# Chunked delta rule: preparing the next head block by block, in the order in which the last head's scan frees its tiles

## The chip, the cores and the metric

One of the eight cores of a Trainium2 chip runs the whole program in one launch. The metric is the device time of one execution in microseconds. TensorE (PE in the profile) multiplies matrices into the eight banks of PSUM; VectorE (DVE), ScalarE (ACT) and GpSimdE (POOL) do elementwise work; SyncE (SP) issues the DMAs.

## What is computed

The reference is a backbone of two layers over 256 context tokens and 1024 latent tokens, model width 1024, all in float32. Each layer has a mixer (one input projection, three groups of heads, one output projection) and a squared-ReLU MLP of width 4096. The three groups are a gated delta rule (GDN, four heads of 128, both directions), an RG-LRU (a linear recurrence, both directions) and latent attention (four heads). The change is in the GDN, which the reference computes like this for each head and direction:

```
G = jnp.cumsum(g, axis=-1)
decay = jnp.exp(jnp.where(incl, G[..., :, None] - G[..., None, :], -jnp.inf))
low = jnp.where(strict, jnp.einsum('nbhid,nbhjd->nbhij', kb, k) * decay, 0.0)
amat = low + jnp.eye(GDN_CHUNK, dtype=low.dtype)
sol = lax.linalg.triangular_solve(amat, rhs, left_side=True, lower=True, unit_diagonal=True)
attn = jnp.einsum('nbhid,nbhjd->nbhij', q, k) * decay
qg = q * jnp.exp(G)[..., None]

def step(S, inp):
    u_i, w_i, a_i, qg_i, kg_i, gl_i = inp
    v_new = u_i - jnp.einsum('bhcd,bhde->bhce', w_i, S)
    o_i = jnp.einsum('bhcd,bhde->bhce', qg_i, S) + jnp.einsum('bhij,bhje->bhie', a_i, v_new)
    S = S * gl_i[..., None, None] + jnp.einsum('bhcd,bhce->bhde', kg_i, v_new)
    return S, o_i
```

## The kernel before

The kernel cuts the 1280 tokens into three blocks: `c` (256 context tokens), 0 and 1 (512 each). For the GDN it uses chunks of 128 tokens, ten of them: 0 and 1 are block `c`, 2 to 5 block 0, 6 to 9 block 1. It is written as straight Python that traces every instruction; a scheduler then puts each engine's instructions into one fixed queue, roughly by their place in the program and by when it expects their inputs to be ready. On the chip each engine works through its queue in order and waits on semaphores. So the order of work is settled before the run, and an instruction that waits holds back what is queued behind it on its engine.

In the mixer (`mixer`), `tiles(h)` projects k, q, v and the gate z of GDN head h: each projected tile is 24 TensorE matmuls of up to 512 columns for each block (`mm3`, L230), a convolution on VectorE, and transpositions into the bank `st` (L443, L462). k, q and v go to memory. `head(h)` then runs the head. The program order is tiles(0), head(0), tiles(1), head(1), tiles(2), head(2), the two RG-LRU projections, tiles(3), head(3), and last the projections of the latent attention (`kvq`). Then come `mla_open` and `mla_prep` (attention's keys, queries and maxima: L950, L958, L984, in banks `st` and `b`), the RG-LRU (`lru`, 20 segments, L847 in bank `lr`), `mla_attend` (L1014 to L1029) and the output projection.

A head has four stages:

- preparation (`gdn_head`, before `gdn_invert`): for each block the decays of both directions (transpositions L624 into banks `a` and `b`, a masked addition on VectorE, exponentials on ScalarE), k·k (L636) into bank `c`, scaled into the triangles `N`, k·q (L646) into bank `c` again, multiplied into the chunk attention `at`, and q scaled by its decay (`Qg`, on GpSimdE);
- inversion (`gdn_invert`): the triangles of all chunks and both directions together. L676 and copies collect 32x32 diagonal blocks in `C`; L681 transposes `C` into `X` on VectorE; 30 pairs of small VectorE instructions follow, then L690 and the small products of L696;
- scan (`gdn_scan`): ten steps in which both directions advance by a chunk. The forward direction takes chunks 0 to 9, the backward one 1, 0, 9, 8, ..., 2. Each step has five products (L766 to L790, banks `a`, `b` and `c`). The output is summed in `o`, which lies in the buffer of `X`; k in token order lies in that of `C`, the states in that of `X2`;
- output (`gdn_y`): squares, a reciprocal root, scaling, transpositions (L821, banks `a`, `b`, `c`), the product with the gate, a store.

Every large tile of a head (`kT`, `qT`, `vt`, `N0`, `N1`, `at0`, `at1`, `Qg1`, `C`, `X`, `X2`) is taken anew for each head from a single buffer (`g5`, `bufs=1`), so that a head's tile takes the place of the last head's. The tiles `L` of the RG-LRU have 14 buffers; a segment takes five.

Of the kernel before, what the change touches and what calls it, by code (L numbers as in the profile page):

```python
# [7 lines left out]
F32 = mybir.dt.float32  # L8
F32R = mybir.dt.float32r
I32 = mybir.dt.int32  # L10
AF = mybir.ActivationFunctionType
ALU = mybir.AluOpType
# [4 lines left out]
P = 128  # L17
# [3 lines left out]
CTX = 256  # L21
TOK = CTX + SEQ
NCH = TOK // P
# [8 lines left out]
BL = ["c", 0, 1]  # L32
# [11 lines left out]
class Trunk:  # L44
# [540 lines left out]
        self.gv8 = ("G", "nG", "neG", "eGl")  # L585
        self.gv = dict(beta=beta, nbeta=nbeta, G=G, nG=nG, neG=neG, eGl=eGl, bk=bk)

    def g5(self, tag):
        return self.gp.tile([P, TOK], F32, tag=tag, bufs=1, name=self.nm(tag))

    def gdn_head(self, L, h, kss, qss, vd, last):

        nc = self.nc
        (kd, ssk, ktd), (qd, _, _) = kss, qss
        y, t, hv, rt, r2 = [self.small([P, NCH], "hk", 6) for _ in range(5)]
        self.rsqrt(y, ssk, t, hv)
        self.tt(rt, ssk, y, ALU.mult)
        self.tt(r2, y, y, ALU.mult)  # L600
        gv = dict(self.gv)
        hc8 = self.small([P, 3, NCH, 2], "hc8", 2)
        for i, k in enumerate(("nbeta", "beta", "bk")):
            gv[k] = hc8[:, i]
            self.tt(hc8[:, i], self.gv[k][:, :, h:8:4], r2.rearrange("p (c o) -> p c o", o=1).to_broadcast([P, NCH, 2]), ALU.mult)
        qbl = [0, 1] if last else BL
        kT, qT, vt = self.g5("kT"), self.g5("qT"), self.g5("vt").rearrange("p (c d) -> p c d", d=P)
        q0 = CTX if last else 0
        nc.sync.dma_start(kT, kd)
        nc.sync.dma_start(qT[:, q0:], qd[:, q0:])  # L610
        nc.sync.dma_start(vt, vd.rearrange("p (c d) -> p c d", d=P))
        self.tt(vt, vt, rt.rearrange("p (c o) -> p c o", o=1).to_broadcast([P, NCH, P]), ALU.mult, nc.gpsimd)
        N = [self.g5(f"N{d}").rearrange("p (c i) -> p c i", i=P) for d in range(2)]
        at = [self.g5(f"at{d}").rearrange("p (c i) -> p c i", i=P) for d in range(2)]
        Qg = [qT, self.g5("Qg1")]
        for b in BL:
            c0, w = GRP[b]
            qs = slice(c0 * P, (c0 + w) * P)
            x = None
            for d in range(2):  # L620
                hc = 4 * d + h
                bc = self.PT("ab"[d]).rearrange("p (c i) -> p c i", i=P)
                for i in range(w):
                    nc.tensor.transpose(bc[:, i, :], gv["G"][:, c0 + i, hc:hc + 1].to_broadcast([P, P]), self.ident)  # L624
                E = at[d][:, c0:c0 + w, :]
                self.tt(E, bc[:, 0:w, :], self.mask[d].rearrange("p (o i) -> p o i", o=1).to_broadcast([P, w, P]), ALU.add)
                for i in range(w):
                    self.act(E[:, i, :], E[:, i, :], AF.Exp, bias=gv["nG"][:, c0 + i, hc:hc + 1])
                if b in qbl:
                    if d == 0:  # L630
                        x = self.T()[:, :w * P]
                    self.act(Qg[1][:, qs] if d else x, bc[:, 0:w, :].rearrange("p c i -> p (c i)"), AF.Exp)
            pk = self.PT("c").rearrange("p (c i) -> p c i", i=P)
            for i in range(w):
                cs = slice((c0 + i) * P, (c0 + i + 1) * P)
                nc.tensor.matmul(pk[:, i, :], kT[:, cs], kT[:, cs], start=True, stop=True)  # L636
            for i in range(w):
                for d in range(2):
                    hc = 4 * d + h
                    c = c0 + i  # L640
                    self.stt(N[d][:, c, :], pk[:, i, :], gv["nbeta"][:, c, d:d + 1], at[d][:, c, :], ALU.mult, ALU.mult)
            if b in qbl:
                pq = self.PT("c").rearrange("p (c i) -> p c i", i=P)
                for i in range(w):
                    cs = slice((c0 + i) * P, (c0 + i + 1) * P)
                    nc.tensor.matmul(pq[:, i, :], kT[:, cs], qT[:, cs], start=True, stop=True)  # L646
                for d in range(2):
                    self.tt(at[d][:, c0:c0 + w, :], pq[:, 0:w, :], at[d][:, c0:c0 + w, :], ALU.mult)
                self.tt(Qg[1][:, qs], qT[:, qs], Qg[1][:, qs], ALU.mult, nc.gpsimd)
                self.tt(qT[:, qs], qT[:, qs], x, ALU.mult, nc.gpsimd)  # L650
        self.gdn_invert(N)
        return self.gdn_scan(h, gv, kT, ktd, vt, N, at, Qg, last)

# [5 lines left out]

    def gdn_invert(self, N):  # L660

# [7 lines left out]
        for a in range(4):  # L669
            q = slice(32 * a, 32 * a + 32)  # L670
            self.cp2(a, C[q, 0:NCH, :], N[0][q, :, 32 * a:32 * a + 32])
        pc = self.PT('a').rearrange("p (c i) -> p c i", i=32)
        for a in range(4):
            q = slice(32 * a, 32 * a + 32)
            for c in range(NCH):
                nc.tensor.matmul(pc[q, c, :], N[1][q, c, 32 * a:32 * a + 32], self.ident[q, 32 * a:32 * a + 32],  # L676
                                 start=True, stop=True, tile_position=(32 * a, 32 * a))
# [148 lines left out]
    def lru(self, L, xd, gd, blocks, yd):  # L826

        nc = self.nc
        gp = nc.gpsimd
        hd = [self.dram(f"lh{t}") for t in range(2)]  # L830
        W = 256
# [1 line left out]
        y0 = GRP[blocks[0]][0] * P  # L833

        def R():
            return self.mp.tile([P, W], F32, tag="L", bufs=14, name=self.nm("lr"))
        prev = {}

        def segment(d, t, b):
            i = 2 * d + t  # L840
            ini = prev.get((d, t), 0.0)
            cs = slice(b * W, (b + 1) * W)
            u = R()
            nc.sync.dma_start(u, xd[t][:, cs])
            ps = self.PT("lr").rearrange("p (g n) -> p g n", g=2)
            for g in range(2):
                nc.tensor.matmul(ps[:, g, :], self.lw[:, d, g, t, :], u, start=True, stop=True)  # L847
            r, wh, y, q = R(), R(), R(), R()

            self.act(r, ps[:, 0, :], AF.Exp, bias=L.col("lba", i))  # L850
# [184 lines left out]
    def mixer(self, L, hs, obl):  # L1035

        nc = self.nc
        l, last = L.l, L.l == DEPTH - 1
        pk = {}
# [4 lines left out]
        d = pk["krba"] = self.dram("krba")  # L1044
# [21 lines left out]
        gp = self.gp = self.pool("gp", other)  # L1066
        self.XAT = gp.tile([P, NCH, 64], F32, name=self.nm("XAT"))
        nc.gpsimd.memset(self.XAT, 0.0)
        kd, xg = [], []

        def tiles(h):
# [362 lines left out]
```

## Time and profile before

| what | us |
|---|---|
| median of three runs | 3839.47 |
| fastest and slowest of them | 3834.44, 3847.36 |
| the profiled execution, its own time | 3835.08 |
| its span, first to last instruction | 3833.3 |
| TensorE busy (91% of the span) | 3505.4 |
| VectorE busy (55%) | 2106.1 |
| ScalarE busy (43%) | 1648.3 |
| GpSimdE busy (34%) | 1314.7 |

The profile is of one execution. A line of its timeline gives the start in us from the span's start, the duration, the engine, the line of the program, the operation, the tiles (written, then read), the shapes, a count of merged instructions and, in brackets, the idle time before it and what ended it. A line of its groups gives a count, the busy time, the mean duration in ns, and the idle time ahead of the group with its causes. PSUM banks appear as `pa`, `pb`, `pc`, `pd`, `pst`, `plr` and `mm`. A float32 product of 128x128 by 128x128 shows as two records. The ends of matmuls are modelled, so that a busy TensorE may in part be a waiting one.

### The profile page before, as it was taken

What the parts mean: (1) busy time and instruction counts of PE and PEld (TensorE: products, weight loads), DVE (VectorE), ACT (ScalarE), POOL (GpSimd) and SP (SyncE); (2) the same over time, 40 slices, a digit from 0 to 9 for tenths busy, and PEclk for the clock granted to TensorE, in tenths of its full rate; (3) what the DMA queues carried; (4) which work ended last, traced back from release to release, by engine and by line L of the source; (5) the groups of instructions that cost most, each with busy time, mean ns of one, the idle gap of its engine ahead of it and who ended that gap; (6) DMA issues with size and microseconds to landing.
All of it is one profiled execution on the core that took longest, in us unless ns stands there. A gap on an engine that the chain in (4) does not pass through costs nothing. (4 is left out here: it accounts for less than half of the span.)

```text
span 3833.3 us, 51463 instructions
## 1 busy us (share of the span) xinstructions
PE 3505.4 (91%) x19236; PEld 2741.0 (72%) x19236; DVE 2106.1 (55%) x4351; ACT 1648.3 (43%) x3477; POOL 1314.7 (34%) x919
## 2 busy tenths in 40 slices
PE   5999898798998999999997989996798999999998
PEld 3777687344687888888877777774455778888886
DVE  6667757666265155555266587677576371421124
ACT  3555464455454322212354455544555453222242
POOL 4211311335475211111466321113334674222253
PEclk9999999898999999999998999997798999999998
DMA  5221222232432222232334222212002433311143
GB/s 182 94 83 66 83 97 76 91 100 64 151 105 88 67 83 94 88 94 89 128 109 138 99 81 82 77 65 87 31 24 74 153 107 94 96 47 46 52 139 99
DMA packets 164922, 347.13 MB, mean 91 GB/s; under 512 B 15552, under 2 KB 74304, under 8 KB 164672
## 3 DMA queue, kind: packets, MB, share of 16 engines
q1 hardware_dynamic: 164672, 343.85, 27.6%
q8 instruction: 151, 2.47, 0.3%
q14 instruction: 99, 0.81, 0.1%
HBM read 277.99 MB, written 65.80 MB: 90 GB/s over the span
## 5 line engine op out<-in xcount | busy, mean ns | idle before, releaser
L138 POOL TENSOR_TENSOR wl<-wr,wh 128x1024 fp32r<-128x1024 f32 x280 | 679.9, 2429 | 1664.2 <-ACT wh L135 931.0
L230 PE MATMUL mm<-A,wh 128*128 128x512 f32 (+1 forms) x3008 | 709.9, 379 | 12.3 <-DVE A L138 6.3
L135 ACT ACTIVATE wh<-wr 128x1024 fp32r<-128x1024 f32 x288 | 304.8, 1058 | 833.0 <-PE mm L230 328.1
L230 PEld LDWEIGHTS mm<-A,wh 128*128 128x128 f32 x3008 | 522.9, 194 | 108.0 <-ACT A L135 8.1
L138 DVE TENSOR_TENSOR hid<-T,hid 128x512 fp32r<-128x512 f32 (+1 forms) x160 | 173.1, 1084 | 448.4 <-ACT hid L135 448.4
L230 PE MATMUL mm<-A,wl 128*128 128x512 f32 (+1 forms) x1504 | 360.8, 373 | 1.5 <-DVE wl L138 1.4
L230 PE MATMUL mm<-hid,wh 128*128 128x512 f32 (+1 forms) x1280 | 302.9, 378 | 8.8 <-ACT T L135 6.8
L230 PEld LDWEIGHTS mm<-A,wl 128*128 128x128 f32 x1504 | 259.8, 191 | 48.0 <-DVE wl L138 1.6
L230 PEld LDWEIGHTS mm<-hid,wh 128*128 128x128 f32 x1280 | 227.8, 191 | 57.1 <-ACT T L135 7.3
L147 DVE SCALAR_TENSOR_TENSOR T<-raw,sm,T 128x512 f32<-128x512 f32 (+4 forms) x240 | 182.1, 760 | 45.4 <-ACT raw L135 24.2
L138 DVE TENSOR_TENSOR acc<-acc,mm 128x512 f32<-128x512 f32 (+1 forms) x140 | 88.5, 632 | 214.9 <-PE mm L230 214.2
L230 PE MATMUL pd<-A,wh 128*128 128x512 f32 (+1 forms) x704 | 193.9, 403 | 0.0
L230 PE MATMUL plr<-A,wh 128*128 128x512 f32 (+1 forms) x800 | 185.2, 382 | 0.0
L135 ACT ACTIVATE T<-T 128x512 f32<-128x512 f32 (+1 forms) x243 | 141.6, 583 | 95.2 <-DVE T L147 69.2
L1029 PE MATMUL pd<-Pt,V 128*128 128x512 f32 (+1 forms) x336 | 170.0, 628 | 10.6 <-ACT Pt L135 9.0
L138 POOL TENSOR_TENSOR S<-S,T 128x512 f32<-128x512 f32 (+1 forms) x126 | 163.4, 1299 | 36.7 <-ACT T L135 33.0
L230 PE MATMUL mm<-hid,wl 128*128 128x512 f32 (+1 forms) x640 | 167.2, 379 | 8.1 <-DVE wl L138 8.1
L230 PE MATMUL pb<-A,wh 128*128 128x512 f32 (+1 forms) x800 | 173.0, 367 | 1.2 <-ACT wh L135 1.2
L147 DVE SCALAR_TENSOR_TENSOR ada<-wa,sil,ada 128x256 f32<-128x256 f32 x392 | 168.4, 493 | 7.1 <-DMA wa<-in_w_ada_dram 7.1
L230 PEld LDWEIGHTS plr<-A,wh 128*128 128x128 f32 x800 | 143.6, 188 | 31.2
L230 PE MATMUL plr<-hid,wh 128*128 128x512 f32 (+1 forms) x640 | 153.4, 381 | 13.0 <-DVE hid L138 9.9
L147 DVE SCALAR_TENSOR_TENSOR lr<-lr,lr 128x256 f32<-128x256 f32 x218 | 107.0, 501 | 96.7 <-POOL lr L138 87.6
(365 smaller groups left out, 6843.5 us busy)
## 6 DMA issues: line engine op xcount, KB each, us to landing
wr<-in_w_mlp_dram SPq DMA_DIRECT2D x208, 512.0 KB, 3.5
wa<-in_w_ada_dram SPq DMA_DIRECT2D x96, 512.0 KB, 3.7
wr<-in_w_in_dram SPq DMA_DIRECT2D x48, 512.0 KB, 3.6
wr<-in_w_out_dram SPq DMA_DIRECT2D x32, 512.0 KB, 3.7
A<-y SPq DMA_DIRECT2D x32, 256.0 KB, 3.2
xm<-acc SPq DMA_DIRECT2D x32, 256.0 KB, 3.5
x<-xm SPq DMA_DIRECT2D x16, 512.0 KB, 6.2
kT<-k SPq DMA_DIRECT2D x8, 640.0 KB, 4.2
```

What stands on the lines that cost most here:

```text
L135: return self.nc.scalar.activation(out, in_, f, **kw)
L138: return (eng or self.nc.vector).tensor_tensor(out, a, b, op=op)
L147: return self.nc.vector.scalar_tensor_tensor(out, a, s, b, op0=op0, op1=op1)
L230: mm = nc.tensor.matmul(ps, w[wi][:, wk, :], a[:, ai, :], start=n == 0, stop=n == last)
L1029: nc.tensor.matmul(po, V[:, c, :], p, start=ci == 0, stop=ci == len(chunks) - 1)
```

## The change

The triangles `N`, the chunk attention `at` and the scaled queries `Qg` become tiles of the whole mixer, taken once for each layer and used by all four heads. A head's preparation is cut into six units, one for each block and direction, and these are written in the order (c, forward), (c, backward), (0, forward), (1, backward), (0, backward), (1, forward). Each unit loads its own part of q into `Qg`, makes its decays in bank `lr`, its own k·k in bank `st` and its own k·q in bank `lr`; before, k·k and k·q were made once for both directions. `kT` gets two buffers, `vt` is loaded and scaled after the units, and the RG-LRU's tiles have 10 buffers in place of 14.

```diff
-    def g5(self, tag):
-        return self.gp.tile([P, TOK], F32, tag=tag, bufs=1, name=self.nm(tag))
+    def g5(self, tag, bufs=1):
+        return self.gp.tile([P, TOK], F32, tag=tag, bufs=bufs, name=self.nm(tag))
...
-        kT, qT, vt = self.g5("kT"), self.g5("qT"), self.g5("vt").rearrange("p (c d) -> p c d", d=P)
...
-        nc.sync.dma_start(kT, kd)
-        nc.sync.dma_start(qT[:, q0:], qd[:, q0:])
-        nc.sync.dma_start(vt, vd.rearrange("p (c d) -> p c d", d=P))
...
-        Qg = [qT, self.g5("Qg1")]
-        for b in BL:
...
-                bc = self.PT("ab"[d]).rearrange("p (c i) -> p c i", i=P)
...
-            pk = self.PT("c").rearrange("p (c i) -> p c i", i=P)
...
-                pq = self.PT("c").rearrange("p (c i) -> p c i", i=P)
...
+        kT, vt = self.g5("kT", 2), self.g5("vt").rearrange("p (c d) -> p c d", d=P)
+        N, at, Qg = self.gNAQ
+
+        def unit(b, d):
+
             c0, w = GRP[b]
             qs = slice(c0 * P, (c0 + w) * P)
+            hc = 4 * d + h
+            if b in qbl:
+                nc.sync.dma_start(Qg[d][:, qs], qd[:, qs])
+            bc = self.PT("lr").rearrange("p (c i) -> p c i", i=P)
+            for i in range(w):
+                nc.tensor.transpose(bc[:, i, :], gv["G"][:, c0 + i, hc:hc + 1].to_broadcast([P, P]), self.ident)
+            E = at[d][:, c0:c0 + w, :]
+            self.tt(E, bc[:, 0:w, :], self.mask[d].rearrange("p (o i) -> p o i", o=1).to_broadcast([P, w, P]), ALU.add)
+            for i in range(w):
+                self.act(E[:, i, :], E[:, i, :], AF.Exp, bias=gv["nG"][:, c0 + i, hc:hc + 1])
+            if b in qbl:
+                x = self.T()[:, :w * P]
+                self.act(x, bc[:, 0:w, :].rearrange("p c i -> p (c i)"), AF.Exp)
+            pk = self.PT("st").rearrange("p (c i) -> p c i", i=P)
             for i in range(w):
                 cs = slice((c0 + i) * P, (c0 + i + 1) * P)
                 nc.tensor.matmul(pk[:, i, :], kT[:, cs], kT[:, cs], start=True, stop=True)
             for i in range(w):
+                c = c0 + i
+                self.stt(N[d][:, c, :], pk[:, i, :], gv["nbeta"][:, c, d:d + 1], at[d][:, c, :], ALU.mult, ALU.mult)
             if b in qbl:
+                pq = self.PT("lr").rearrange("p (c i) -> p c i", i=P)
                 for i in range(w):
                     cs = slice((c0 + i) * P, (c0 + i + 1) * P)
+                    nc.tensor.matmul(pq[:, i, :], kT[:, cs], Qg[d][:, cs], start=True, stop=True)
+                self.tt(E, pq[:, 0:w, :], E, ALU.mult)
+                self.tt(Qg[d][:, qs], Qg[d][:, qs], x, ALU.mult, nc.gpsimd)
+        nc.sync.dma_start(kT, kd)
+
+        for b, d in (("c", 0), ("c", 1), (0, 0), (1, 1), (0, 1), (1, 0)):
+            unit(b, d)
+        nc.sync.dma_start(vt, vd.rearrange("p (c d) -> p c d", d=P))
+        self.tt(vt, vt, rt.rearrange("p (c o) -> p c o", o=1).to_broadcast([P, NCH, P]), ALU.mult, nc.gpsimd)
         self.gdn_invert(N)
...
-            return self.mp.tile([P, W], F32, tag="L", bufs=14, name=self.nm("lr"))
+            return self.mp.tile([P, W], F32, tag="L", bufs=10, name=self.nm("lr"))
...
+        self.gNAQ = [[self.g5(f"{k}{d}") for d in range(2)] for k in ("N", "at", "Qg")]
+        self.gNAQ[:2] = [[t.rearrange("p (c i) -> p c i", i=P) for t in ts] for ts in self.gNAQ[:2]]
```

More of the change, by code (lines that the diff above doesn't have):

```diff
@@ L606, in gdn_head @@
         qbl = [0, 1] if last else BL
-        kT, qT, vt = self.g5("kT"), self.g5("qT"), self.g5("vt").rearrange("p (c d) -> p c d", d=P)
-        q0 = CTX if last else 0
-        nc.sync.dma_start(kT, kd)
-        nc.sync.dma_start(qT[:, q0:], qd[:, q0:])
-        nc.sync.dma_start(vt, vd.rearrange("p (c d) -> p c d", d=P))
-        self.tt(vt, vt, rt.rearrange("p (c o) -> p c o", o=1).to_broadcast([P, NCH, P]), ALU.mult, nc.gpsimd)
-        N = [self.g5(f"N{d}").rearrange("p (c i) -> p c i", i=P) for d in range(2)]
@@ L614, in gdn_head @@
-        at = [self.g5(f"at{d}").rearrange("p (c i) -> p c i", i=P) for d in range(2)]
-        Qg = [qT, self.g5("Qg1")]
-        for b in BL:
+        kT, vt = self.g5("kT", 2), self.g5("vt").rearrange("p (c d) -> p c d", d=P)
+        N, at, Qg = self.gNAQ
+        def unit(b, d):
             c0, w = GRP[b]
             qs = slice(c0 * P, (c0 + w) * P)
-            x = None
-            for d in range(2):
-                hc = 4 * d + h
-                bc = self.PT("ab"[d]).rearrange("p (c i) -> p c i", i=P)
[L623 to L632, printed above, removed]
-            pk = self.PT("c").rearrange("p (c i) -> p c i", i=P)
@@ L637, in gdn_head @@
             for i in range(w):
[L638 to L641, printed above, removed]
+                c = c0 + i
+                self.stt(N[d][:, c, :], pk[:, i, :], gv["nbeta"][:, c, d:d + 1], at[d][:, c, :], ALU.mult, ALU.mult)
             if b in qbl:
-                pq = self.PT("c").rearrange("p (c i) -> p c i", i=P)
+                pq = self.PT("lr").rearrange("p (c i) -> p c i", i=P)
                 for i in range(w):
                     cs = slice((c0 + i) * P, (c0 + i + 1) * P)
[L646 to L650, printed above, removed]
+                    nc.tensor.matmul(pq[:, i, :], kT[:, cs], Qg[d][:, cs], start=True, stop=True)
[6 more added lines that the diff above has]
+        self.tt(vt, vt, rt.rearrange("p (c o) -> p c o", o=1).to_broadcast([P, NCH, P]), ALU.mult, nc.gpsimd)
         self.gdn_invert(N)
```

## The prediction

> **What bounds the kernel now.** I read the page first: the engines' shares, then the forty slices.
>
> ```profile
> span 3833.3 us, 51463 instructions
> PE 3505.4 (91%) x19236; PEld 2741.0 (72%) x19236; DVE 2106.1 (55%) x4351; ACT 1648.3 (43%) x3477; POOL 1314.7 (34%) x919
> ...
> PE   5999898798998999999997989996798999999998
> ```
>
> TensorE (PE) is busy 91% of the span, and, counting slices of 95.8 us from 0, its dips lie in 4 to 12 and 21 to 30, the deepest in 27 and 28: the mixers of layer 0 and layer 1, where the four GDN heads run one after another. The rest is projection matmuls back to back, which the change doesn't touch. So I read the mixers stage by stage, in the timeline, for where the scan of one head ends (the last sum into `o`, DVE L138 `X<-X,pc`) and where the inversion of the next begins (the DVE transposition L681).
>
> ```profile
> 2321.81 0.29 DVE L138 TENSOR_TENSOR X<-X,pc 128x128 f32<-128x128 f32 x1 [1.17 <-PE pc L790]
> 2337.38 0.41 PE L821 MATMUL pb<-cst,X 128*128 128x128 f32 x1
> 2337.58 0.64 PE L624 MATMUL pa<-cst,gv 128*128 128x128 f32 x2
> 2357.75 2.09 DVE L681 STREAM_TRANSPOSE X<-C 128x1024 f32<-128x1024 f32 x1 [1.05 <-POOL qT L138]
> ...
> 2450.77 0.29 DVE L138 TENSOR_TENSOR X<-X,pc 128x128 f32<-128x128 f32 x1 [0.85 <-PE pc L790]
> 2489.70 2.09 DVE L681 STREAM_TRANSPOSE X<-C 128x1024 f32<-128x1024 f32 x1 [1.06 <-POOL qT L138]
> ...
> 2585.76 0.29 DVE L138 TENSOR_TENSOR X<-X,pc 128x128 f32<-128x128 f32 x1 [0.15 <-PE pc L790]
> 2613.89 2.10 DVE L681 STREAM_TRANSPOSE X<-C 128x1024 f32<-128x1024 f32 x1 [1.06 <-POOL qT L138]
> ```
>
> In layer 1 the gaps from scan to inversion are 36, 39 and 28 us. In the first, the last transposition of `gdn_y` (L821) starts at 2337.38, and the decays of the next head (L624, into bank `a`) only after it: the next head's preparation stands wholly in the gap. What this costs at the end shows in the table of stretches (after the length: busy time of PE, PE's weight loads, DVE, ACT and POOL with the number of instructions, then the granted clock and the DMA share):
>
> ```profile
> 2620.00:2760.00 140.00, 77.64 (x554) 53.94 (x553) 98.35 (x239) 68.64 (x184) 53.05 (x68) 0.70 0.17 55
> 2760.00:2980.00 220.00, 201.33 (x682) 119.94 (x681) 144.76 (x246) 117.05 (x238) 88.43 (x104) 0.93 0.15 46
> ```
>
> While head 3 of layer 1 inverts and scans (2620 to 2760), PE has 77.6 us of work in 140: the projection tiles have run out, and attention waits for the head.
>
> ```profile
> PE pa L821 <- ACT X L135: 12.0, 1, 12.0
> ...
> 2737.61 0.63 PE L950 MATMUL pb<-kvn,wk 128*64 128x256 f32 x1
> ```
>
> Its keys (L950) need bank `b`, which the scan and `gdn_y` of head 3 hold, and resume at 2737.61, behind a transposition of `gdn_y` (L821) that waited 12.0 us for ScalarE at the head of TensorE's queue. There a shorter chain of heads is worth time. In layer 0 it is not so:
>
> ```profile
> 267.49 0.29 DVE L138 TENSOR_TENSOR X<-X,pc 128x128 f32<-128x128 f32 x1 [1.39 <-PE pc L790]
> 304.33 2.09 DVE L681 STREAM_TRANSPOSE X<-C 128x1024 f32<-128x1024 f32 x1 [1.05 <-POOL qT L138]
> ...
> 521.78 0.29 DVE L138 TENSOR_TENSOR X<-X,pc 128x128 f32<-128x128 f32 x1 [0.22 <-PE pc L790]
> 562.15 0.38 PE L624 MATMUL pa<-cst,gv 128*128 128x128 f32 x2
> ```
>
> Head 2 ends at 522 and head 3 begins at 562: for 40 us no head runs, since its projections (`tiles(3)`) aren't there.
>
> **The change, part by part.**
>
> *The gap.* Four of six units (block and direction) can run while the last scan still works on the others, if a tile's parts are freed one by one. For reading this is so already:
>
> ```profile
> 291.06 0.43 PE L676 MATMUL pa<-cst,N 32*32 32x32 f32 x8
> 296.95 2.16 DVE L147 SCALAR_TENSOR_TENSOR N<-pc,hc,at 128x128 f32<-128x128 f32 x8
> ```
>
> L676 reads the first chunks of `N` 6 us before its last ones are written. What stays in the gap is the longer of two things: the units of the last blocks, and the release of `X` (the scan's `o`) by `gdn_y`, 2337.8 − 2321.8 = 16.0 us. I take 18 us for a gap. Gained in layer 1: 18 + 21 + 10 = 49 us. Bounds: 0 if nothing starts early; 103 − 3 × 9 = 76 if `gdn_y` shrinks to half as well.
>
> *The scan.* The moved units lengthen it. Groups of instructions (count, busy us, mean ns), and the stretch of one scan:
>
> ```profile
> L147 DVE SCALAR_TENSOR_TENSOR N<-pc,hc,at 128x128 f32<-128x128 f32 x160 | 44.0, 343 | 10.9 <-PE pc L636 8.6 <-ACT at L135 1.1 <-ACT Qg L135 0.9
> L135 ACT ACTIVATE at<-at,gv 128x128 f32<-128x128 f32 x160 | 51.7, 391 | 11.4 <-DVE at L138 11.3
> L138 DVE TENSOR_TENSOR at<-pc,at 128x512 f32<-128x512 f32 (+1 forms) x40 | 23.6, 631 | 14.3 <-PE pc L646 14.2
> L138 DVE TENSOR_TENSOR at<-pa,cst 128x512 f32<-128x512 f32 (+1 forms) x24 | 14.3, 594 | 10.9 <-PE pa L624 10.9
> L135 ACT ACTIVATE T<-pa 128x512 f32<-128x512 f32 (+1 forms) x20 | 10.7, 537 | 0.0
> ...
> 2288.60:2321.80 33.20, 33.20 (x230) 29.57 (x231) 16.38 (x47) 16.60 (x51) 2.79 (x2) 1.00 0.14 35
> ```
>
> Four units are 12 chunks: on DVE 12 × 0.343 + 4 × (0.631 + 0.594) = 9.0 us, on ACT 12 × 0.391 + 4 × 0.537 = 6.8 us. Each engine is busy half of the scan (16.4 and 16.6 of 33.2), so most of the 15.8 us falls into idle time; I take 5 us a scan, 15 for three, between 0 and 47.
>
> *Doubled products.* k·k and k·q are made once for each direction: 160 + 144 PE records more.
>
> ```profile
> 295.87 1.05 PE L636 MATMUL pc<-kT 128*128 128x128 f32 x8
> ...
> L636 PE MATMUL pc<-kT 128*128 128x128 f32 x160 | 22.8, 281 | 1.2 <-DVE at L138 1.0
> L646 PE MATMUL pc<-qT,kT 128*128 128x128 f32 x144 | 19.3, 275 | 0.0
> ```
>
> Eight follow each other in 1.05 us, the last lasting 0.28: 0.11 us each, 33.5 us for 304. Inside a scan they are covered: PE is busy there by the profile, but mostly with waiting, as its projection matmuls (L230) show in the stretches of that line alone:
>
> ```profile
> 2288.60:2321.80 33.20, 19.39 (x54) 9.45 (x55) 1.00 0.14 35
> 2321.80:2357.80 36.00, 23.57 (x75) 14.03 (x75) 0.91 0.30 108
> ...
> 267.80:304.30 36.50, 26.12 (x111) 17.19 (x110) 1.00 0.38 142
> 522.10:561.90 39.80, 33.95 (x161) 26.52 (x160) 1.00 0.40 136
> ```
>
> 54 in 33 us of scan against 161 in 39.8 us alone. If that cover is gone, all 33.5 us count.
>
> *One bank in place of two.* Decays and k·q now share `lr`, k·k has `st`, which the projection tiles use too. A head with no scan before it (head 0; head 3 of layer 0) makes its units one behind the other: the bank is held by the addition, the exponential and the product, 0.594 + 0.537 + 0.631 = 1.8 us by their groups above, so some 2 us more for each of the three blocks: 6 us (an estimate), between 0 and 12. In layer 1 that is +6 on the chain.
>
> The decays of before do alternate between banks `a` and `b`, and a row of L624 above writes `a`. The Trainium skill, "Perfetto Trace Analysis", Matmuls, asks for just this: independent matmul groups should rotate through different PSUM banks, so that one is emptied while the next is filled. By that rule every head's preparation would grow as head 0's does, 8 × 6 = 48 us in place of the 10 that the sum below charges, and the result would be 3823 + 38 = 3861, about where rival C ends. No run shown here has the one-bank form.
>
> *Loads.* q comes in 6 pieces (4 in layer 1) for each head in place of one, 32 issues more on SP.
>
> ```profile
> L610 SPq DMA_DIRECT2D qT<-q x8: 319/351/457, 130.2 to 2584.8; - x8
> DMA to landing us min/median/max: 3.4/5.3/6.8
> ```
>
> At 0.35 us that is 11 us of SP over eight heads. A piece waits for the scan's last read of its part, and weight loads queue behind it; since it lands within 5.3 us and k·q is wanted only by the scan, I put this at 0, at most one landing a head on PE (8 × 5.3 = 42) if PE reaches k·q first. `kT` with two buffers can load during the last scan, and `vt`, now asked for after the units, is first needed by the scan, so the whole inversion covers it: 0 for both; without that cover `vt` would cost its landing, some 5 us by the row of q, a head.
>
> *RG-LRU's buffers, 14 to 10.* A segment takes five tiles, so 10 still hold two segments, and two is what the queue of SP shows, each next load issued right behind a store of the segment two before:
>
> ```profile
> 2688.64 0.32 SPq L883 DMA_DIRECT2D lh<-lr  x1
> 2689.06 0.38 SPq L844 DMA_DIRECT2D lr<-lx  x1
> ```
>
> I take 0; at worst each of 20 segments waits for that store to land, 3.4 us by the quickest landing in the row of q: 0 to 68 us, beside attention.
>
> *To the end of layer 1.* At head 3's end the chain is 49 − 15 − 6 = 28 us earlier. But RG-LRU then loses alone-time: the tiles that ran in the gaps (75 L230 in 36 us) still have to run, so it starts some 9 us later, and attention 28 us earlier; at 15 us a segment (20 loads issued in 290.7 us) about three segments move into attention.
>
> ```profile
> L844 SPq DMA_DIRECT2D lr<-lx x20: 319/410/608, 2628.9 to 2919.6; - x20
> 2760.00:2980.00 220.00, 12.28 (x44) 7.88 (x44) 46.03 (x101) 44.72 (x100) 69.15 (x90) 0.93 0.15 46
> ```
>
> The second row counts only RG-LRU's instructions: 11 segments (44 PE records, four each) cost DVE 46.0 us, 4.2 each, and DVE is 66% busy there (144.8 of 220): 0.66 × 4.2 × 3 = 8 us. So −20 us at the end of layer 1, between −28 and 0.
>
> *Layer 0.* Heads 0 to 2 end about 23 us earlier (two gaps, 19 and 20, less two scans at 5 and 6 for head 0), but the 40 us without a head show that this waits for projections. Two gaps give up 39 us at 111 L230 in 36.5 us, 118 records, of which the longer scans and head 0's preparation take back some 32; 86 records at 161 in 39.8 us are 21 us. So `tiles(3)` comes out even, and head 3's 6 us, partly beside the last projections, leave +4, between −15 and +12.
>
> The sum: −20 + 4 = −16 us against the profiled execution's 3835.08, 3819. That execution is 4.4 below the median of 3839.47, so the median goes to 3823, 0.43% faster. About 0.3% (11.5 us) is what a measurement of this kernel can tell from no change.
>
> **The rivals.**
>
> *A: all of it arrives.* If scans don't stretch and layer 0's tiles keep pace, layer 1 gives −35 and layer 0 −10: about 3794. For it: DVE and ACT idle half of each scan. Against it: the 40 us of layer 0 without a head.
>
> *B: the gain is given back.* Head 3 ends earlier, but RG-LRU ends when it did, and the last loads for the output projection wait for it: layer 1 at −3, layer 0 at +4, about 3840, no change. For it: the 290.7 us of its loads reach to 2919.6, 60 us before attention ends at 2980. Against it: its engines are not full.
>
> *C: slower, by the parked bank.* k·k of the next unit needs only `kT`, so it can be put into `st` long before the scan frees its part of `at`, and sit there. Then the projection tiles' transpositions, which have no bank but `st`, wait, and TensorE in order behind them. Units of the third and fourth place wait for step 5 of ten, the last two for step 9: up to 25 us a scan. At 54 L230 lost per 33 us of scan and 161 regained per 39.8, 25 us cost 10 us a head, 60 for six heads; about 40 where tiles decide, against the 20 of layer 1: near 3860. It decides from about 8 us of parking a scan, where its 3 us for each of six heads eat the 16. For it: `st` is the tiles' only bank. Against it: tiles of the next head are done before its units.
>
> *D: the parts aren't freed one by one,* and nothing starts early: head 0's 6 us for eight heads less what is hidden, +25: 3865. Against it: L676 above.
>
> **How the numbers follow.** The forecast (3805 to 3828) gets 0.40, A 0.12, B 0.24, C 0.17, D 0.07. Faster: 0.52; no change: 0.24; slower: 0.24. The likeliest is the forecast, 3823. The range reaches to A and C, 3790 to 3862; the forecast's own is 3805 to 3828.
>
> **What would show it.** Right: k·k of the next head between L770s of the last scan; the gaps in layer 1 near 18 us; scans near 38; L950 resuming near 2710; head 3 of layer 0 starting where it did. Wrong: gaps as long as before (D); PE waits on the tiles' transpositions that grow in the scans (C); attention starting earlier and the output projection not (B). What would upset the sum most is the order that a new static schedule gives to in-order queues: one wait like L821's is 12 us.

## The result: 0.9% slower, and the profile after

The changed kernel takes 3876.27 us, the kernel before 3840.22 us on the same chip: ratio 1.0090, 95% interval 1.0075 to 1.0105. Forecast were 3823 us, 0.43% faster, and a range to 3862; the time lies above the range. The profiled execution of the changed kernel took 3874.43 us, with a span of 3872.7. Its page, the same rows as shown of before:

```profile
span 3872.7 us, 52200 instructions
PE 3542.8 (91%) x19540; PEld 2778.6 (72%) x19540; DVE 2103.4 (54%) x4351; ACT 1646.4 (43%) x3477; POOL 1311.4 (34%) x919
...
PE   5999989798999999999997989997698999999998
```

The second set of products is there, 304 more records on PE (19540 against 19236; two records are one product), the other engines are as they were, and the dips of the slices still lie in the two mixers. So the loss has to be found by stage. In the line numbers of the changed kernel everything behind the new `gdn_head` stands four lines higher (L681 is L677, and so on); its k·k is L630, its k·q L638, its decays L619.

*The gaps of layer 1*, from the last sum of a scan into `o` to the start of the inversion (timeline of VectorE, changed kernel):

```profile
2361.22 0.29 DVE L138 TENSOR_TENSOR X<-X,pc 128x128 f32<-128x128 f32 x1 [1.17 <-PE pc L786]
2396.55 2.03 DVE L677 STREAM_TRANSPOSE X<-C 128x1024 f32<-128x1024 f32 x1 [0.79 <-ACT C L135]
...
2492.55 0.29 DVE L138 TENSOR_TENSOR X<-X,pc 128x128 f32<-128x128 f32 x1 [1.41 <-PE pc L786]
2529.16 2.03 DVE L677 STREAM_TRANSPOSE X<-C 128x1024 f32<-128x1024 f32 x1 [0.79 <-ACT C L135]
...
2622.64 0.29 DVE L138 TENSOR_TENSOR X<-X,pc 128x128 f32<-128x128 f32 x1 [1.17 <-PE pc L786]
2656.36 1.92 DVE L677 STREAM_TRANSPOSE X<-C 128x1024 f32<-128x1024 f32 x1
```

35.3, 36.6 and 33.7 us, where 18 were forecast and 36, 39 and 28 stood before: nothing is gained. The reason shows in the first scan of layer 0, which runs to 277 us (timeline, first unit of the next head):

```profile
256.77 0.38 PE L619 MATMUL plr<-cst,gv 128*128 128x128 f32 x2
257.18 0.43 DVE L138 TENSOR_TENSOR at<-plr,cst 128x256 f32<-128x256 f32 x1 [1.15 <-PE plr L619]
260.16 0.59 DVE L147 SCALAR_TENSOR_TENSOR N<-pst,hc,at 128x128 f32<-128x128 f32 x2
261.07 0.61 PE L630 MATMUL pst<-kT 128*128 128x128 f32 x4
...
281.15 0.19 ACT L135 ACTIVATION_READ_ACCUMULATOR T<-X 128x1 f32 x1
281.36 0.32 SPq L814 DMA_DIRECT2D T<-z  x1
290.07 0.38 SPq L814 DMA_DIRECT2D T<-z  x1
293.42 0.38 ACT L135 ACTIVATE T<-plr 128x256 f32<-128x256 f32 x1
293.85 0.71 PE L638 MATMUL plr<-Qg,kT 128*128 128x128 f32 x4
...
298.31 0.64 DVE L147 SCALAR_TENSOR_TENSOR N<-pst,hc,at 128x128 f32<-128x128 f32 x2 [0.47 <-ACT at L135]
```

The unit starts in the scan as it should: decays at 256.77, mask at 257.18, `N` at 260.16, so the parts of `at` and `N` are freed one by one. Then its exponential `x` (`T<-plr`) comes 36 us later. `x` takes one of two scratch tiles of the head's actor, and `gdn_y` of the last head holds these for its squares (to 281.15) and its `z` (loads issued at 281.36 and 290.07); e1 below tests whether it is this wait. Until `x` has read it, bank `lr` is parked, and behind it all other units; the k·k of the second unit sits in bank `st` from 261.07 to 298.31, when its `N` is made. The units then follow each other in the gap.

*Layer 0* lost more. The last transposition of head 3's projection tiles (L462) and the first decays behind it, before and after, and the projection matmuls (L230) in the stretch up to there (length, busy time of PE with the count, weight loads, granted clock, DMA share):

```profile
554.19 0.65 PE L462 MATMUL pst<-cst,T 128*128 128x128 f32 x4
...
58.00:554.80 496.80, 347.88 (x1481) 246.89 (x1482) 0.96 0.24 82
```

```profile
570.26 0.66 PE L462 MATMUL pst<-cst,T 128*128 128x128 f32 x4
578.22 0.38 PE L619 MATMUL plr<-cst,gv 128*128 128x128 f32 x2
...
58.00:570.90 512.90, 343.86 (x1481) 247.76 (x1482) 0.97 0.26 84
```

In both kernels exactly 1481 projection records stand ahead of head 3, and head 3 follows the last transposition by some 7 us. The same projections take 16.1 us longer. Between them stand the products of heads 0 to 2 (groups of TensorE by form in the same stretches, before and after):

```profile
L636 PE MATMUL pc<-kT 128*128 128x128 f32 x60 | 8.5, 280 | 1.1 <-DVE at L138 1.0
L646 PE MATMUL pc<-qT,kT 128*128 128x128 f32 x60 | 8.2, 275 | 0.0
```

```profile
L630 PE MATMUL pst<-kT 128*128 128x128 f32 x120 | 17.2, 277 | 0.3 <-DVE N L147 0.3
L638 PE MATMUL plr<-Qg,kT 128*128 128x128 f32 x120 | 17.1, 282 | 1.2 <-ACT T L135 1.2
```

120 records more at the prediction's 0.11 us are 13.2 of the 16.1 us. Head 3 itself then runs into RG-LRU. RG-LRU's matmuls within its scan (the stretch runs from the scan's first product to the end of its last sum into `o`), before and after:

```profile
626.70:666.20 39.50, 2.22 (x8) 1.29 (x8) 1.00 0.37 123
```

```profile
654.20:703.50 49.30, 4.14 (x12) 2.02 (x12) 0.93 0.24 74
```

Twelve RG-LRU matmuls in place of eight, the first 19 us into the scan in place of 31, and a scan of 49.3 in place of 39.5 us. Attention of layer 0 starts at 751.7 in place of 723.2 and, of the same length, ends 28.6 us later.

### The profile page after: what moved, and what is told of

The parts are those of the page before. It is cut to its first block, busy times and chain, and to the rows that moved or that the text cites. A ratio compares the mean times of both kernels' runs of the same rounds, so it can differ in the third digit from the quotient of the medians.

```text
span 3872.7 us, 52200 instructions
## 1 busy us (share of the span) xinstructions
PE 3542.8 (91%) x19540; PEld 2778.6 (72%) x19540; DVE 2103.4 (54%) x4351; ACT 1646.4 (43%) x3477; POOL 1311.4 (34%) x919
## 3 DMA queue, kind: packets, MB, share of 16 engines
q1 hardware_dynamic: 169280, 348.57, 28.1%
## 5 line engine op out<-in xcount | busy, mean ns | idle before, releaser
L230 PE MATMUL mm<-A,wh 128*128 128x512 f32 (+1 forms) x3008 | 703.9, 376 | 15.2 <-DVE A L138 7.7
L230 PEld LDWEIGHTS mm<-A,wh 128*128 128x128 f32 x3008 | 520.6, 192 | 111.3 <-DVE A L138 9.2
L230 PE MATMUL mm<-A,wl 128*128 128x512 f32 (+1 forms) x1504 | 352.9, 372 | 1.4 <-DVE wl L138 1.4
L230 PE MATMUL mm<-hid,wh 128*128 128x512 f32 (+1 forms) x1280 | 302.2, 377 | 5.7 <-ACT T L135 4.0
L230 PEld LDWEIGHTS mm<-A,wl 128*128 128x128 f32 x1504 | 260.4, 191 | 49.6 <-DVE wl L138 1.6
L230 PEld LDWEIGHTS mm<-hid,wh 128*128 128x128 f32 x1280 | 227.9, 191 | 53.1 <-ACT T L135 4.4
L230 PE MATMUL pd<-A,wh 128*128 128x512 f32 (+1 forms) x704 | 197.4, 411 | 1.5 <-ACT T L135 1.0
L1025 PE MATMUL pd<-Pt,V 128*128 128x512 f32 (+1 forms) x336 | 166.7, 617 | 21.1 <-ACT Pt L135 13.8
L230 PE MATMUL plr<-A,wh 128*128 128x512 f32 (+1 forms) x800 | 185.3, 383 | 0.0
L230 PE MATMUL mm<-hid,wl 128*128 128x512 f32 (+1 forms) x640 | 166.9, 379 | 8.1 <-DVE wl L138 8.1
L230 PE MATMUL pb<-A,wh 128*128 128x512 f32 (+1 forms) x800 | 173.0, 367 | 1.2 <-ACT wh L135 1.2
L230 PEld LDWEIGHTS plr<-A,wh 128*128 128x128 f32 x800 | 143.6, 188 | 31.3
L230 PE MATMUL plr<-hid,wh 128*128 128x512 f32 (+1 forms) x640 | 153.2, 381 | 12.8 <-DVE hid L138 10.0
L230 PEld LDWEIGHTS pb<-A,wh 128*128 128x128 f32 x800 | 136.8, 190 | 27.5 <-ACT wh L135 1.3
```

The source lines that it names most:

```text
L230: mm = nc.tensor.matmul(ps, w[wi][:, wk, :], a[:, ai, :], start=n == 0, stop=n == last)
L1025: nc.tensor.matmul(po, V[:, c, :], p, start=ci == 0, stop=ci == len(chunks) - 1)
```

## Experiments

All times are ratios to the kernel before on the same chip, and 0.1% is 3.8 us. The stages are read from one profile each. Layer 0 is the same code in before, e9, e14 and e15, and its attention ended at 1003.4, 1003.5, 1008.6 and 1013.0 us: in layer 0 a difference under 10 us between two profiles says nothing by itself. In the table, "head 3" is the first decay of head 3 in layer 0, "end 0" the last value product of layer 0's attention, and layer 1 is counted from a mark shortly ahead of it, the last long wait in layer 0's MLP (the product `mm<-hid,wl` that starts after 8 us of idle TensorE, at 2080.9 before), to the first score of attention, and from there to the last value product.

| kernel | ratio | head 3 | end 0 | layer 1: to attention + attention = sum |
|---|---|---|---|---|
| before | 1 | 562.2 | 1003.4 | 680.3 + 219.3 = 899.6 |
| after | 1.0090 | 578.2 | 1032.0 | 689.2 + 219.6 = 908.8 |
| e1 own x | 1.0095 | 579.8 | 1033.9 | 666.2 + 240.0 = 906.2 |
| e2 doubled only | 1.0066 | 580.1 | 1029.9 | 663.2 + 239.5 = 902.7 |
| e3 buffers only | 1.0012 | 562.2 | 1005.6 | 680.0 + 220.8 = 900.8 |
| e4 own x, banks a, b, c | 1.0081 | 586.9 | 1044.2 | 654.4 + 239.9 = 894.3 |
| e5 after, single | 1.0129 | 587.1 | 1044.2 | 692.3 + 219.9 = 912.2 |
| e6 own x, single | 1.0040 | 577.7 | 1036.5 | 639.3 + 238.2 = 877.5 |
| e7 tiles(3) first | 1.0002 | 540.0 | 1017.5 | 665.1 + 229.1 = 894.2 |
| e8 e4 with tiles(3) first | 1.0054 | 528.3 | 1034.2 | 631.3 + 265.5 = 896.8 |
| e9 shared, layer 1 | 0.9970 | 561.0 | 1003.5 | 642.5 + 239.6 = 882.1 |
| e10 shared, both layers | 1.0019 | 573.4 | 1033.0 | 642.8 + 240.7 = 883.5 |
| e11 no products | 1.0037 | 571.7 | 1012.9 | 678.7 + 218.6 = 897.3 |
| e12 loads only | 1.0007 | 566.1 | 1011.9 | 679.1 + 217.9 = 897.0 |
| e13 own x, bank lr | 1.0150 | 580.7 | 1047.4 | 681.2 + 237.6 = 918.8 |
| e14 change in layer 1 | 1.0033 | 562.9 | 1008.6 | 686.6 + 221.6 = 908.2 |
| e15 e9 with tiles(3) first | 0.9902 | 568.0 | 1013.0 | 620.9 + 236.9 = 857.8 |

**e1: the exponential in a tile of its own**

```diff
-                x = self.T()[:, :w * P]
+                x = self.tp.tile([P, 512], F32, tag="ada", bufs=1, name=self.nm("xu"))[:, :w * P]
```

> The changed kernel, but the exponential that scales q (x in a unit) gets a tile of its own (a buffer that only the MLP stage uses) in place of one of the two scratch tiles that the head's output stage also takes. Theory T (scratch): in the changed kernel x waits for the last head's output stage to give up a scratch tile, and bank lr stays taken meanwhile, so nothing but the first unit starts in the scan. Then here the units move into the scans, the gaps from scan to inversion fall from 44, 43 (layer 0) and 35, 37, 34 us (layer 1) to 25 or less, and the time falls from 3876 to 3825-3848. Theory O (one bank and doubled products): the units themselves got slower; gaps stay at 33 to 45 and the time within 8 us of 3876.

Ratio 1.0095 (1.0078 to 1.0112), no faster. The mechanism is confirmed and its worth is not: the units now run within the scans and the first gaps of layer 1 fall to 22.7 and 22.0 us, but head 3's grows to 41.8, since its projection tiles come late (timelines of VectorE and of TensorE):

```profile
2365.07 0.28 DVE L138 TENSOR_TENSOR X<-X,pc 128x128 f32<-128x128 f32 x1
2387.72 2.01 DVE L677 STREAM_TRANSPOSE X<-C 128x1024 f32<-128x1024 f32 x1
```

```profile
2606.11 0.66 PE L462 MATMUL pst<-cst,T 128*128 128x128 f32 x4
2611.98 0.38 PE L619 MATMUL plr<-cst,gv 128*128 128x128 f32 x2
```

The scan of head 2 had ended at 2596.3. The head waited for its tiles, not for the scan.

**e2: every k·k and k·q product of the kernel before made twice, e3: RG-LRU's tiles from 14 to 10, each alone**

```diff
-                nc.tensor.matmul(pk[:, i, :], ...)
+                for _ in range(2):
+                    nc.tensor.matmul(pk[:, i, :], ...)
```

> The kernel before with one thing alone: each k.k and k.q product is made twice (304 more TensorE records, same banks, same results). Theory O: 20 to 33 us slower than before (304 x 0.11 us mostly on the path). Theory T: 0 to 10 us slower, since the projection matmuls wait about anyway in these stretches.

> The kernel before with one thing alone: the RG-LRU's tiles have 10 buffers in place of 14. Theories T and O both: within 5 us of before. A third theory L (the RG-LRU with two segments and no spare tile falls behind attention): 8 us slower or more, with the last segment's matmuls and the end of attention later in both layers.

e2: 1.0066 (1.0051 to 1.0081), 25 us, of which the layers show 26.5 by the end of layer 0 and 3 in layer 1. Head 3 of layer 0 starts 18 us late, as after the change, and its projections (L230, the stretch of above) take 514.8 in place of 496.8 us at the same granted clock:

```profile
58.00:572.80 514.80, 352.02 (x1481) 249.47 (x1482) 0.96 0.23 79
```

The program of this kernel is otherwise that of before, so the second products by themselves cost 25 of the 36 us that the change lost. e3: 1.0012 (1.0002 to 1.0023), 4.6 us.

**e4: own x, and the units of heads that have no scan beside them in banks a, b and c**

```diff
-            bc = self.PT("lr").rearrange(...)
+            bc = self.PT("ab"[d] if free else "lr").rearrange(...)   # k·k and k·q: "c" if free
```

> As the first of these (own tile for x), and besides, the heads that have no scan beside them (head 0 of both layers, head 3 of layer 0) make their units in the banks of before (decays in a and b, products in c). Theory T, with the bank's price of about 6 to 8 us for each of these heads: 8 to 20 us faster than the run with its own x tile. Theory O: their preparation shrinks from 28 to 36 us to 21 to 25, and the time falls by 10 to 20 us against 3876, but the gaps stay.

1.0081 (1.0067 to 1.0095), 5 us below e1, within the intervals of the two. Head 0's preparation, first decay to inversion, goes from 28.8 to 27.2 us in layer 0 and from 36.9 to 27.5 in layer 1. Head 3 of layer 0 gains nothing (28.1 and 28.6). So the single bank costs 0 to 9 us a head; before the change the three took 21.1, 23.4 and 21.4, and the rest comes with the other parts, the second set of products and the units' order, not told apart here.

**e5 and e6: the changed kernel and e1 without the second products**

```diff
+            second = (b, d) in (("c", 1), (0, 1), (1, 0))
-            pk = self.PT("st").rearrange(...)
+            pk = kT[:, qs].rearrange(...) if second else self.PT("st").rearrange(...)
-            for i in range(w):
+            for i in range(0 if second else w):
                 nc.tensor.matmul(pk[:, i, :], ...)
...              # pq in the same way, from Qg[d]
```

> The changed kernel, in which the second unit of each block does not make its k·k and k·q products (152 products of TensorE for each direction's second use, 304 in all, so as many as in the kernel before); its N and `at` are made from k and q themselves, so the numbers differ and the time is that of the order alone. Theory W (the products are work that TensorE has no room for): doubling cost 24 us in the kernel before, so leaving it out brings the changed kernel from ratio 1.009 to about 1.003. Rival S (the loss comes from the shared scratch tiles and the parked banks, and the products hide in the waits these make): the ratio stays at 1.007 or more.

> The same without the second products, with the exponential x in a tile of its own (as in the run e1_own_x, 1.0095). Theory W: 1.0095 less 24 us, about 1.003; if the shorter gaps are worth what the prediction said (20 us), these now show, and the ratio falls below 1.000. Rival S: 1.007 or more.

e5: 1.0129 (1.0115 to 1.0144), slower with less work than the changed kernel; rival S's bound holds, but neither theory has a loss that grows. e6: 1.0040 (1.0027 to 1.0054), between the two theories. In layer 1 e6 takes 877.5 us, 22 less than before: about the 20 us of the prediction, with its two obstacles taken away (the second units here need no bank for products either). In layer 0 nothing comes back. The projections up to head 3 there, in e6:

```profile
58.00:570.40 512.40, 338.94 (x1481) 251.79 (x1482) 0.94 0.26 85
```

As many products as before, the same 1481 projections, and still 15.6 us more than before's 496.8, with a granted clock of 0.94 against 0.96. Length times granted clock is an estimate of what the stretch would take at full clock, to some 3 us by the rounding of the clock, and takes all of the slower clock as lost time: 477 us before, 498 after the change (0.97), 494 in e2, 482 here. So some 10 of the 15.6 us go with the lower clock, while the 18 and 16 us of e2 and of the changed kernel do not.

**e7 and e8: head 3's projections ahead of RG-LRU's inputs, in the kernel before and in e4**

```diff
-        xtile(0)
-        xtile(1)
         tiles(3)
         head(3)
+        xtile(0)
+        xtile(1)
         kvq()
```

> The kernel before with the projections of head 3 put ahead of RG-LRU's two inputs in the program (tiles(3) and head(3) before xtile). Theory W (TensorE's work sets the end of the mixers): head 3 of layer 0 starts up to 40 us earlier, but RG-LRU starts later and the same projections still have to run; the time stays within 12 us of the kernel before. Rival H (the chain of heads sets the end): 20 to 40 us faster, most of it by an earlier end of attention in layer 0.

> The run e4_own_x_ab (own tile for x; heads with no scan beside them use banks a, b and c), with tiles(3) and head(3) ahead of RG-LRU's inputs. In e4 head 3 waits for its projections in both layers. Theory W: the wait goes, the heads end 30 to 50 us earlier, and the time stays near e4's 1.008. Rival H: 20 to 50 us faster than e4, a ratio of 0.995 to 1.003.

e7: 1.0002 (0.9994 to 1.0011); head 3 of layer 0 starts 22 us earlier and attention 13 us later. In layer 0 an earlier head 3, paid for with later RG-LRU inputs, is worth nothing: theory W's figure holds. e8: 1.0054 (1.0041 to 1.0068), 10 us below e4 and between the two theories. Head 3's last scan ends 17 us earlier than before in layer 0 and 68 us earlier in layer 1 (from the mark), but attention of layer 1 starts only 49 us earlier and takes back 46 of them.

**e9 and e10: decays early by block and direction, products made once per block, in layer 1 and in both**

```diff
+        for b, d in (("c", 0), ("c", 1), (0, 0), (1, 1), (0, 1), (1, 0)):
+            x = unit(b, d)                      # q, decays, mask, exponentials
+            if (b, d) in (("c", 1), (0, 1), (1, 0)):
+                products(b, d, x)               # k·k and k·q once, for N and at of both directions
```

k·k of blocks 0 and 1 goes to bank `c`, everything else of a unit to `lr`, so `st` stays with the tiles; head 0, which has no scan beside it, uses `a`, `b` and `c` as in e4; `x` has its own tile, and RG-LRU ten tiles in the layers that are changed.

> Layer 0 as in the kernel before. In layer 1 the decays of a next head are made by block and direction as in the changed kernel (x in a tile of its own), but each block's k·k and k·q are made once, when the later of its two directions is free, so TensorE has no more products than before. Theory W (doubled products and waits lengthen the projections of layer 0, a shorter gap is worth something in layer 1 only): layer 0 as before, layer 1 between 899.6 us (before) and 877.5 (the run e6_own_x_single): 5 to 20 us faster than the kernel before, ratio 0.995 to 0.999. Rival G (what the heads gain is given back by RG-LRU beside attention): attention starts earlier and lasts as much longer, ratio 0.999 to 1.002.

> The same in both layers. Theory W: layer 0 has no doubled products, but the waits at the head of TensorE's queue grow as in e6_own_x_single (head 3 of layer 0 starts 10 to 15 us late), so layer 0 loses 10 to 30 us and the ratio is 1.000 to 1.006. If layer 0 loses by the doubled products alone, it stays even and the ratio is that of e9_shared_l1.

e9: 0.9970 (0.9960 to 0.9981), 11.5 us faster than the kernel before. In its profile, its fastest execution, layer 1 takes 882.1 us, 17.5 less than before; attention starts 37.8 us earlier and lasts 20.3 longer, so theory W's range and rival G's mechanism are both seen, G at half its size. e10: 1.0019 (1.0009 to 1.0028). With no product doubled, layer 0 still loses 30 us, so doubling is not layer 0's only cause.

**e11: the kernel before without any k·k or k·q product, e12: only the loads of q by block and of v behind them**

```diff
-            pk = self.PT("c").rearrange(...)
+            pk = kT[:, qs].rearrange(...)          # e11; pq from qT in the same way, no matmuls
...
-        nc.sync.dma_start(qT[:, q0:], qd[:, q0:])  # e12; vt with its multiplication to behind the blocks
+            if b in qbl:
+                nc.sync.dma_start(qT[:, qs], qd[:, qs])
```

> The kernel before without any k·k and k·q (N and `at` are made from k and q themselves; 304 products of TensorE are left out). Theory W: in layer 0 every product of TensorE stands in front of the projections, so tiles(3) is done 12 us earlier (120 products of 0.11 us) and head 3 starts near 550 in place of 562; the whole is 15 to 30 us faster, ratio 0.992 to 0.996. Rival (the prediction's: products are covered by waits): 562 within 3 us, ratio 0.998 to 1.000 but for what the chain of a head itself gains, 4 us a head.

> The kernel before with one part of the change alone: q loaded by block, and v after the blocks in place of before them. Prediction and theory W: nothing, ratio within 0.3% of 1. A rival by which any other order of the queues costs layer 0 some 15 us (head 3 started 13 to 25 us late in six of eight changed kernels, with very different changes): ratio 1.003 to 1.006 here too.

e11: 1.0037 (1.0024 to 1.0050), slower with 304 records less, and head 3 of layer 0 starts at 571.7 in place of 550. Neither expectation comes out. Its projections up to head 3:

```profile
56.60:564.40 507.80, 356.34 (x1481) 256.19 (x1482) 0.93 0.24 80
```

The stretch is 11 us longer than before, at a granted clock of 0.93 against 0.96. By the estimate of e6 it would take 472 us at full clock, against 477 before: 5 us less, in theory W's direction and under half of its 12 us. So e11 does not show that products are free; it shows a slower clock. That is so in every execution, by the clock granted over the whole of each: 0.948 to 0.951 in the six of e11, against 0.955 to 0.962 in the 26 of before on that chip. In e5 it is 0.949 to 0.953, against 0.954 to 0.961 in its 17. The changed kernel has 0.956 to 0.962, like before, so its own loss is not the clock's. Why the clock is lower in e5 and e11 no run shows.

e12: 1.0007 (0.9993 to 1.0020), so loading by block costs nothing (the second load of q for each direction isn't in it), and not every new order of the queues costs layer 0 time.

**e13: e1 with k·k in bank lr in place of st**

```diff
-            pk = self.PT("st").rearrange(...)
+            pk = self.PT("lr").rearrange(...)
```

> The run e1_own_x with one line changed: k·k goes to bank lr in place of st, so the projection tiles have st to themselves; the products stay doubled. Rival C of the prediction (the parked bank): the last transposition of v for head 3 of layer 1 ends near 2570 in place of 2606.8, the gap before head 3 falls from 42 to under 30 us, and layer 1 (first projection to the end of attention) takes 875 to 890 us in place of 906. Theory W (the products' own work): it stays at 900 to 910.

1.0150 (1.0136 to 1.0164), 21 us worse than e1. The experiment does not settle rival C: the last v tile of head 3 ends 466 us after the mark in place of 494 in e1, so `st` did hold the tiles up, but decays, k·k and k·q of a unit now wait for each other in one bank. At the first gap of layer 1 (timelines of TensorE and VectorE):

```profile
2387.64 0.60 PE L619 MATMUL plr<-cst,gv 128*128 128x128 f32 x4
...
2388.32 0.28 DVE L138 TENSOR_TENSOR X<-X,pc 128x128 f32<-128x128 f32 x1
2423.72 2.06 DVE L677 STREAM_TRANSPOSE X<-C 128x1024 f32<-128x1024 f32 x1
```

The gap is 35.4 us again. The rule of the Trainium skill, "Perfetto Trace Analysis", Matmuls, that independent matmul groups should rotate through banks, which the prediction weighed, agrees with this trace: 35.4 us with one bank for a unit, 22.7 with two in e1. The 21 us of the whole are not the price of the bank alone, since the clock granted here is 0.951 to 0.954, against 0.952 to 0.962 in e1, and `st` became free.

**e14: the change as it is, in layer 1 alone**

```diff
+        if last:
+            ...                                    # gdn_head of the changed kernel
         kT, qT, vt = self.g5("kT"), ...            # gdn_head of the kernel before
```

> The change as it is in layer 1, with layer 0 as in the kernel before. If the layers' losses are independent, layer 0 ends attention at 1003 ± 3 and layer 1 takes 909 ± 5 us against 899.6: ratio 1.001 to 1.004. If layer 1's loss came from layer 0 (another order of the queues after it), the ratio is 0.998 to 1.001.

1.0033 (1.0022 to 1.0045), and layer 1 takes 908.2 us against 908.8 in the changed kernel. The layers' losses are independent to within the noise: 0.33% are layer 1's, the remaining 0.57% layer 0's.

**e15: e9 with tiles(3) and head(3) ahead of RG-LRU's inputs in layer 1** (the edit of e7, in that layer alone)

> The run e9_shared_l1 with tiles(3) and head(3) ahead of RG-LRU's inputs in layer 1. Head 3's gap falls from 31 to some 20 us and attention starts up to 10 us earlier. Rival G (given back): RG-LRU, whose inputs come later, then runs more segments beside attention, which gets as much longer; the ratio stays at 0.996 to 0.999. If the heads set the end: 0.994 to 0.996.

0.9902 (0.9887 to 0.9918): 36 us faster than the kernel before, more than either expectation. All three gaps are now what the prediction had taken, 19.4, 18.2 and 19.8 us:

```profile
2339.56 0.29 DVE L138 TENSOR_TENSOR X<-X,pc 128x128 f32<-128x128 f32 x1 [0.87 <-PE pc L849]
2358.92 2.06 DVE L740 STREAM_TRANSPOSE X<-C 128x1024 f32<-128x1024 f32 x1 [0.45 <-issue]
...
2453.34 0.29 DVE L138 TENSOR_TENSOR X<-X,pc 128x128 f32<-128x128 f32 x1 [0.61 <-PE pc L849]
2471.55 2.10 DVE L740 STREAM_TRANSPOSE X<-C 128x1024 f32<-128x1024 f32 x1 [0.73 <-ACT C L135]
...
2560.89 0.29 DVE L138 TENSOR_TENSOR X<-X,pc 128x128 f32<-128x128 f32 x1 [0.86 <-PE pc L849]
2580.68 2.03 DVE L740 STREAM_TRANSPOSE X<-C 128x1024 f32<-128x1024 f32 x1 [0.57 <-ACT C L135]
```

The two edits are worth 17.5 us (e9) and 5.4 us (e7's layer 1) alone and 41.8 together, by one profile each; by whole times e9 gains 11.5 and e15 36. It fits that neither pays while the other of the two, the scan or head 3's tiles, is late. A part may be the clock, 0.962 to 0.965 in e15 against 0.957 to 0.959 before. RG-LRU's matmuls beside attention of layer 1, before and in e15 (the stretch is attention):

```profile
2761.20:2980.50 219.30, 12.28 (x44) 7.88 (x44) 0.94 0.16 47
```

```profile
2716.50:2953.40 236.90, 17.08 (x60) 11.20 (x60) 0.93 0.16 47
```

With 15 segments beside it in place of 11 attention is 17.6 us longer, and it still ends 41.8 us earlier, because it starts 59.4 us earlier. The number of segments alone does not set its length: e9 has 13 beside it (52 records) and is 20.3 us longer.

## Why the prediction was wrong, by its own steps

*The gap (−49).* Half right. That four units can run in the scan, and that parts of a tile are freed one by one, is seen. The floor of 18 us was right: 19.4, 18.2 and 19.8 in e15. The step overlooked that a unit needs a third thing besides `at`/`N` and a bank: the scratch tile of `x`, which `gdn_y` holds to the end of the gap. In the changed kernel 0 of the 49 us came (rival D's outcome by another cause).

*The scan (+15).* Too dear. Scans with the units in them take 33.9, 35.2 and 35.4 us in e15 against 33.2, 36.4 and 35.4 before: nothing.

*Doubled products (0).* The term that was mis-sized, and the larger part of the 36 us lost. "Inside a scan they are covered" took the waits that PE's busy time hides for room; but the queue is in order, and each product stands in front of a projection. In layer 0 the 1481 projections ahead of head 3 took 16.1 us longer, 13.2 of them the price of 120 records. Alone (e2) the second products cost 25 us, near the 33.5 named as the price without cover. Taking products out gave back less than that, or nothing, in e5 and e11; there the granted clock fell, which by the estimate of e6 hides 5 us of gain in e11's layer 0. That the 25 us are all work of the products is not shown.

*One bank for heads without a scan (+6 each).* About right: e4 gives 0, 2 and 9 us. The preparation of these heads grew by more in the changed kernel, by 7 to 13 us, from the other causes as well.

*Loads (0) and RG-LRU's buffers (0).* Right for the loads as far as e12 has them (1.0007), nearly so for the buffers (1.0012, 1 to 9 us by its interval).

*The end of layer 1 (−20).* Right in size once the obstacles are gone (−22 in e6, −17.5 in e9), for terms that were both too small: attention starts 38 to 41 us earlier, not 28, and 19 to 20 us are given back, not 8. With two segments more beside it attention is 20.3 us longer in e9, where the step took 2.8 us for each; what else lengthens it is not shown. In the changed kernel it was +9.

*Layer 0 (+4).* This failed most: +28.6. That layer 0 waits for projections was read rightly from the 40 us without a head, and e7 fits it. But then every microsecond added on TensorE counts, and a head 3 that starts 16 us late meets RG-LRU. Its scan takes 34.7 us in e7 and 35.4 in e8 with no RG-LRU matmul in it, 39.5 before with eight, 49.3 after and 49.4 in e1 with 12, 52.8 in e10 and 51.3 in e13 with 16 (e2 and e4, with four, 39.8 and 42.8). The row of e7:

```profile
617.10:651.80 34.70, 0.00 (x0) 0.00 (x0) 1.00 0.02 5
```

That RG-LRU is what stretches it is read from these, not tried by itself. Nor is it shown that the scan's end is what holds attention: in e7 it came 14 us earlier than before, and attention started 13 us later.

*The signs.* k·k of a next head between the scan's matmuls is seen (261.07); the keys (L950 before, L946 now) resumed at 2770, not 2710, and head 3 of layer 0 started 16 us late.

*Rivals.* D came nearest in time (3865) and in what the gaps show, but not by its cause, since parts are freed one by one. C had the sign too, near 3860. Its mechanism, k·k parked in `st`, is in the trace (261 to 298 us) and e13 freed the tiles by 28 us, but its price couldn't be told from that of one bank. B's give-back is real and grows with the gain: 46 of 49 us in e8.

What stays open is why the granted clock is lower in e5, e11 and e13, and what makes up the loss of layer 0 in e10, where no product is doubled (30 us, of which head 3's start is 11).

## What to carry to other kernels

Before work is pulled into another stage's shadow, list every resource it takes, scratch tiles too, and who holds each till when; one forgotten buffer kept the gaps of layer 1 as long as before. Where an in-order engine is the bound, an instruction that looks covered can cost its length (25 us here, 33.5 by length), so early work should be the decays that sit on other engines, and shared matmuls stay shared. Two waits that end together are best taken away together: 17.5 and 5.4 us of layer 1 alone were 41.8 as a pair. And look at the granted clock before a loss is put down to the order of work.

## What the runs showed of the hardware

Leaving out 304 matmul records made the kernel 0.37% slower, with a granted clock of 0.948 to 0.951 over the whole in place of 0.955 to 0.962. In the stretch ahead of head 3 length times clock orders the kernels by their products where length alone does not: 472 us with none (e11, 507.8 long), 477 and 482 with one set (before, 496.8; e6, 512.4), 494 and 498 with two (e2, 514.8; after, 512.9). And the same code of layer 0 ended its attention anywhere from 1003.4 to 1013.0 us in four kernels that differ only later, which is the limit of what one profile can tell.
